# Hybrid MLA and forgetting attention block: latents and their weights as fp16 halves with scales found on the chip, and one weight tile loaded in the opening

## The chip, the cores and the metric

The kernel runs on one core of a Trainium2 chip. The metric is the device time of one launch in microseconds (us). Before the change three runs took 578.58, 579.78 and 581.6 us, median 579.78.

## The reference

One decoder layer over 16 meta tokens and 512 real ones, model width 1024, in fp32. Two attention branches read the same normalised input; their gated outputs go through one projection.

```python
u = rmsnorm(h, pre_norm_g)
(cq, ckv, k_pe_raw, z_mla, fq, fk, fv, f_logit, z_fox, gate_a, gate_b) = split(u @ w_in)
q  = rmsnorm(cq,  mla_q_norm_g)  @ w_uq    # 256 -> 16 heads x (64 nope + 32 rope)
kv = rmsnorm(ckv, mla_kv_norm_g) @ w_ukv   # 128 -> 16 heads x (64 key + 64 value)
# MLA: rope on q's and k's 32 columns, causal softmax, heads of 64
y_mla = (attention(q_m, k_m, v_mla) * silu(z_mla)) @ w_br_mla
# FoX: 16 heads of 64, logits plus cum[t] - cum[s], cum = cumsum(log_sigmoid(f_logit + b))
y_fox = (attention(fq, fk, fv, cum) * silu(z_fox)) @ w_br_fox
h = h + rmsnorm((sigmoid(gate_a) * y_mla + sigmoid(gate_b) * y_fox) @ w_out, post_norm_g)
```

The products on which the change works are the two with `w_uq` and `w_ukv`: `cq` and `ckv` are the latent tokens.

## The kernel before

Every fp32 product is made of three passes on halves: upper by upper, upper by lower, lower by upper (`passes`, L279). A half is either float32r (the upper half a cast, the lower a subtraction, `split_lo` L109) or fp16. Where it is fp16, the weight is brought into range by a scale found on the chip: class `Halved` (L232) loads a tile of 128x1024 (`wraw`), takes a bound of its values (`peak`: on ScalarE an `Abs` pass into `junk` with a sum, on VectorE a `TENSOR_REDUCE`), `scales` (L190) makes powers of two of the bounds of up to three tiles at once with a tiny matmul (`scale`) and a few small VectorE and GpSimd instructions (`sc`), ScalarE writes the upper half, and VectorE in one or GpSimd in two instructions the lower one. `su` holds small constants.

In fp16 are the tokens (`hTh`, `hTl`) and all the weights of `w_in` used in the stages: `z` (gates of the branches), `fq`, `fk`, `v` of FoX, `pg` (merge gates). In float32r are the latents (`cTh`, `cTl`, made in `latent`, L585), the weights of `mq`, `mk` and the MLA `v` (one tile of 128x640, two loads, from `w_uq` and `w_ukv`; `q_mla`, L773), and those of the rope part of the queries (`pe_unit`, L805: group 0 for heads 0 to 7, group 1 for the rest; products `ppe`, four loads of 64-byte rows each).

There are 16 attention stages, two heads each, FoX and MLA in turn: stage 0 is FoX pair 0, stage 1 MLA pair 0, stage 2 FoX pair 1, and so on. A stage makes its scores (`st`) on TensorE, takes masked maxima and exponentials (`sf`) on VectorE and ScalarE, normalised fp16 probabilities (`pn`) on VectorE, ScalarE and GpSimd, has them turned by four DMA transposes (`pt`) and multiplies them with the values (`ov`, 26 matmuls). TensorE's order is written by hand: the scores of the next stage come ahead of the values of this one, and the rest of a stage is filled with products that later stages need. In a FoX stage the fill is `za` (24 matmuls `z` of 512 columns), `mq` (6), `zb` (24), with `mk` (6) and the MLA `v` (6) between; in an MLA stage `fq`, `fk` and `v` (24 each in two parts, `fk` and `v` in 272 and 256 columns) of the next FoX stage. `zs`, `feeds`, `sets` and `fills` (L1144 to 1195) hold these. The other engines follow the order of a scheduler, with `issue_after` and priorities where code sets them.

All loads and transposes stand in one queue on SyncE (SP): an instruction that waits there holds up what follows. In an MLA stage it has loads of `wraw`, the transposed values (`vp`), loads of the MLA weights and `pt`; in a FoX stage the reload of the rope queries (`QP`), two loads, `vp`, two loads of `cbp` (the forget gates' sums) and `pt`. In stages 8 and 10 SP runs through without a break from `QP` to the last `pt`.

The opening, up to about 60 us, norms the tokens, makes the latents, group 0 of `ppe`, and `fq`, `fk` and `v` of stage 0; GpSimd then makes the masks `cbm` (L1111, L1112) for stage 0.

Of the kernel before, what the change touches and what calls it, by code (L numbers as in the profile page):

```python
# [23 lines left out]
S = 512  # L24
# [23 lines left out]
ROW = 16  # L48
# [8 lines left out]
def block_kernel(ctx: ExitStack, tc: tile.TileContext, x, meta_tokens, pre_norm_g, w_in, fox_forget_b,  # L57
# [132 lines left out]
    def scales(ws):  # L190
# [3 lines left out]
        def peak(j):  # L194
            raw = ws[j].load()[1]
# [3 lines left out]
            if on[0] is nc.scalar:  # L199
                with nc.allow_low_precision("a bound that becomes a power of two"):  # L200
                    tc.keep_in_program_order(nc.scalar.activation(junk[0], raw, AF.Abs, accum_out=mp))
# [3 lines left out]
        def run_():  # L205
# [14 lines left out]
            for j, w in enumerate(ws):  # L220
                w.s, w.r = inv[:, j : j + 1], r[:, j : j + 1]

# [50 lines left out]

    def by_k(part, nk):
# [14 lines left out]
    cTh, cTl = (cqk.tile([128, 3, ROW + L - META], F32R, tag=n, name=n)[:, :, ROW - META :] for n in ("cTh", "cTl"))  # L289
# [110 lines left out]

    lctx = ExitStack()
    with ExitStack() as ph:
# [182 lines left out]
        def latent(t, sm):  # L585
# [8 lines left out]
            with tc.high_priority(offset=60):  # L594
                nc.scalar.copy(cTh[:, i0:3, ds], pc[:, i0:3, :rows])
                nc.scalar.copy(KP[0][0:ROPE, ds], pc[0:ROPE, 3, :rows])
                nc.scalar.activation(fT[:, ds], pc[ROPE : ROPE + NH, 3, :rows], AF.Identity, bias=fb)
                split_lo(nc.vector, cTl[:, i0:3, ds], pc[:, i0:3, :rows], cTh[:, i0:3, ds])
                split_lo(nc.vector, KP[1][0:ROPE, ds], pc[0:ROPE, 3, :rows], KP[0][0:ROPE, ds])
# [46 lines left out]
        scaled(4, pin)  # L646
        squares(3, pin)
# [29 lines left out]
        latent(4, sms[4])  # L677
        small(3, three, second_half)
# [14 lines left out]
        nc.vector.scalar_tensor_tensor(out=fa[:, 1], in0=fa[:, 0], scalar=1.0 / SC_FOX, in1=fa[:, 1], op0=ALU.mult, op1=ALU.add)  # L693
        for t in (4, 0, 1):
            narrowed(t, lowered["sm", 3])
        run(qk[7:])
# [26 lines left out]
    with ExitStack() as att:  # L723
# [44 lines left out]
        wuqh = wuq.rearrange("p k (h e) -> p k h e", e=NOPE + ROPE)  # L768

# [3 lines left out]
        def q_mla(pr):  # L773
            ld = []

            def load():
                if not ld:
                    ld.append(wload([wuq[:, :, 192 * pr : 192 * pr + 192], wukv[:, 256 * pr : 256 * pr + 256]], mla_room))

            def get():  # L780
                load()
                u, raw, _, _ = ld[0]
                wh, wl = half_rooms(u)
                cuts = [(raw[:, 0:384].rearrange("p (b e) -> p b e", e=96)[:, :, 0:NOPE], lambda t: t[:, 0:256].rearrange("p (b e) -> p b e", e=NOPE)),
                        (raw[:, 384:640].rearrange("p (h a e) -> p a h e", h=2, a=2), lambda t: t[:, 256:512].rearrange("p (a h e) -> p a h e", a=2, h=2))]
                for src, to in cuts:
# [446 lines left out]
        for x in range(2):  # L1233
            both0(x)
# [477 lines left out]
```

## Time and profile before

| | before |
|---|---|
| median of three runs | 579.78 us (578.58 to 581.6) |
| profiled execution | 580.54 us |
| its span, first to last instruction | 578.8 us |
| mean granted TensorE clock | 0.995 |
| VectorE, ScalarE, GpSimd busy | 468.0, 390.8, 232.1 us |
| HBM read | 62.62 MB |

In the page, PE is TensorE's matmuls, PEld its weight loads, DVE VectorE, ACT ScalarE, POOL GpSimd, SP SyncE. A row of a timeline gives the start, the duration, the engine, the line, the operation, what it writes and reads, the number of instructions, and in brackets the idle time of the engine ahead of it with what ended it. A row of the chain gives start, duration, engine, name, line and number. A row of a grouped view gives the sum and mean duration of a form. A window gives its length, the busy time of each engine (and instructions begun), the granted clock, the mean share of the DMA engines in use and GB/s.

### The profile page before, as it was taken

What the parts mean: (1) busy time and instruction counts of PE and PEld (TensorE: products, weight loads), DVE (VectorE), ACT (ScalarE), POOL (GpSimd) and SP (SyncE); (2) the same over time, 40 slices, a digit from 0 to 9 for tenths busy, and PEclk for the clock granted to TensorE, in tenths of its full rate; (3) what the DMA queues carried; (4) which work ended last, traced back from release to release, by engine and by line L of the source; (5) the groups of instructions that cost most, each with busy time, mean ns of one, the idle gap of its engine ahead of it and who ended that gap; (6) DMA issues with size and microseconds to landing.
All of it is one profiled execution on the core that took longest, in us unless ns stands there. A gap on an engine that the chain in (4) does not pass through costs nothing.

```text
span 578.8 us, 11317 instructions
## 1 busy us (share of the span) xinstructions
PE 563.0 (97%) x3864; PEld 399.8 (69%) x3864; DVE 468.0 (81%) x1251; ACT 390.8 (68%) x859; POOL 232.1 (40%) x346
## 2 busy tenths in 40 slices
PE   8999979999999999999999999999999999999995
PEld 6888656667568668567676676645686675788884
DVE  6868798888878989878888788879958986478966
ACT  7867787787885886976887878864443463343762
POOL 4422823775685597756846756600000000000000
PEclk9999998999999999999999999999999999999999
DMA  8525899889999897997997986658824230323603
GB/s 301 106 56 152 254 175 290 161 210 241 193 223 220 156 200 132 217 228 150 244 247 162 211 183 146 156 102 295 286 74 110 72 110 11 110 99 109 219 0 145
DMA packets 220025, 97.74 MB, mean 169 GB/s; under 512 B 131352, under 2 KB 209568, under 8 KB 219968
## 3 DMA queue, kind: packets, MB, share of 16 engines
q1 hardware_dynamic: 219968, 97.03, 70.1%
q8 instruction: 30, 0.49, 0.3%
q14 instruction: 27, 0.22, 0.1%
HBM read 62.62 MB, written 4.23 MB: 116 GB/s over the span
## 4 chain that ended last, share of the span: by engine, by line
PE 77%; DVE 8%; DMA 5%; ACT 4%; issue 2%; POOL 2%; SPq 1%; DVEq 0%; ACTq 0%; POOLq 0%
PE z L104 15%; PE pg L104 10%; PE py L104 8%; PE fq L104 7%; PE v L104 7%; PE x L104 6%; PE fk L104 6%; PE st L104 5%; PE ov L104 5%; DMA pt<-pn 4%; PE psm L104 2%; PE mq L104 2%; PE y L104 2%; DVE w L269 1%; DVE wl L110 1%
## 5 line engine op out<-in xcount | busy, mean ns | idle before, releaser
L104 PEld LDWEIGHTS <-w 128*128 128x128 f16 x1584 | 150.1, 98 | 114.6 <-issue 4.3
L1014 ACT ACTIVATE sf<-sf,nb 128x272 f32<-128x272 f32 (+3 forms) x128 | 72.7, 568 | 25.3 <-DVE nb L979 23.1
L104 PE MATMUL z<-hTh,w 128*128 128x512 f16 x256 | 81.9, 380 | 0.0
L272 POOL TENSOR_TENSOR w<-wraw,w 128x1024 f16<-128x1024 f32 x35 | 74.9, 2141 | 2.3
L104 PE MATMUL pg<-hTh,w 128*128 128x512 f16 x240 | 72.6, 379 | 0.8 <-DVE w L269 0.8
L1053 DVE SCALAR_TENSOR_TENSOR pn<-sf,ri,pn 128x512 f16<-128x512 f32 (+3 forms) x128 | 70.9, 611 | 1.6 <-ACT pn L1049 1.6
L219 POOL TENSOR_SCALAR sc<-sc,su 128x2 f32<-128x2 f32 (+2 forms) x22 | 8.3, 379 | 146.3 <-DVE sc L216 146.3
L258 ACT ACTIVATE w<-wraw,sc 128x1024 f16<-128x1024 f32 x43 | 48.3, 1144 | 24.2 <-DVE sc L218 18.5
L1049 ACT ACTIVATE pn<-sf,ri 128x128 f16<-128x128 f32 (+3 forms) x128 | 59.6, 547 | 0.5 <-DVE ri L1019 0.5
L104 PE MATMUL z<-hTl,w 128*128 128x512 f16 x128 | 48.5, 379 | 0.0
L110 DVE TENSOR_TENSOR wl<-wraw,w 128x512 fp32r<-128x512 f32 (+1 forms) x44 | 38.4, 880 | 12.2 <-PE scale L104 4.4
L271 POOL TENSOR_SCALAR wraw<-wraw,sc 128x1024 f32<-128x1024 f32 x35 | 39.8, 1136 | 20.5 <-ACT w L258 19.4
L104 PE MATMUL pg<-hTl,w 128*128 128x512 f16 x120 | 45.5, 379 | 0.0
L104 PE MATMUL st<-hlk,hlq 64*128 64x272 f32 (+4 forms) x480 | 41.4, 299 | 0.0
L104 PE MATMUL fk<-hTh,w 128*128 128x272 f16 (+1 forms) x224 | 40.1, 276 | 0.0
L104 PE MATMUL v<-hTh,w 128*128 128x272 f16 (+1 forms) x224 | 39.3, 276 | 0.0
L104 PE MATMUL ov<-pt,vp 128*64 128x512 f16 (+4 forms) x416 | 33.2, 311 | 4.7 <-DMA pt<-pn 4.7
L104 PEld LDWEIGHTS st<-hlk,hlq 64*128 64x128 f32 x480 | 33.1, 186 | 5.8 <-ACT vh L903 2.5
L104 PE MATMUL fq<-hTh,w 128*128 128x512 f16 x112 | 35.2, 386 | 0.0
L104 PEld LDWEIGHTS <-vp 128*64 128x64 f16 (+1 forms) x416 | 22.3, 111 | 17.7 <-issue 6.9
L1415 ACT CAST w<-wraw 128x512 fp32r<-128x512 f32 x28 | 16.7, 617 | 23.1 <-DVE wraw L1424 18.6
L165 ACT CAST w<-wraw 128x1024 fp32r<-128x1024 f32 (+1 forms) x20 | 20.2, 1015 | 17.0 <-PE py L104 15.3
(342 smaller groups left out, 1478.5 us busy)
## 6 DMA issues: line engine op xcount, KB each, us to landing
wraw<-in_w_in_dram SPq DMA_DIRECT2D x47, 512.0 KB
room<-in_w_in_dram SPq DMA_DIRECT2D x9, 512.0 KB
cbp<-c_dram SPq DMA_DIRECT2D x16, 264.0 KB
wraw<-in_w_br_fox_dram SPq DMA_DIRECT2D x8, 512.0 KB
tb<-in_w_out_dram SPq DMA_DIRECT2D x8, 512.0 KB
wraw<-in_w_br_mla_dram SPq DMA_DIRECT2D x8, 512.0 KB
wraw<-in_w_out_dram SPq DMA_DIRECT2D x6, 512.0 KB
QP<-qpe_dram SPq DMA_DIRECT2D x8, 256.0 KB
```

The costliest lines, as they stand in the source:

```text
L104: nc.tensor.matmul(*a, **k)
L110: return eng.tensor_tensor(out=lo, in0=src, in1=f32(hi), op=ALU.subtract)
L165: nc.scalar.copy(wh[:, :n], raw[:, :n])
L219: nc.gpsimd.tensor_scalar(out=r, in0=t, scalar1=su[:, 5:6], scalar2=1.0, op0=ALU.mult, op1=ALU.mult)
L258: self.hi = nc.scalar.activation(hi, raw, AF.Copy, scale=self.s).ins
L269: nc.vector.scalar_tensor_tensor(out=lo, in0=raw, scalar=self.s, in1=hi, op0=ALU.mult, op1=ALU.subtract)
L271: nc.gpsimd.tensor_scalar(out=raw, in0=raw, scalar1=self.s, scalar2=1.0, op0=ALU.mult, op1=ALU.mult)
L272: nc.gpsimd.tensor_tensor(out=lo, in0=raw, in1=hi, op=ALU.subtract)
L1014: exps[b // 3] = nc.scalar.activation(sf, sf, AF.Exp, bias=sums["nb"][:, h, b : b + 1], scale=-1.0, accum_out=sums["su"][:, h, b : b + 1]).ins
L1049: normed[:] = [nc.scalar.activation(hi, sf, AF.Copy, scale=rib).ins]
L1053: nc.vector.scalar_tensor_tensor(out=lo, in0=sf, scalar=rib, in1=hi, op0=ALU.mult, op1=ALU.subtract)
L1415: nc.scalar.copy(to[0], src)
```

## The change

Latents and MLA weights become fp16 halves:

- `latent` writes `cTh` by ScalarE and `cTl` by one VectorE instruction with a scale that is found from the largest gain of the norm (four small VectorE instructions on `su`).
- A class `Parts` on top of `Halved` does the same for the MLA tile (640 columns) and for the rope weights (512): peak, share in a `scale` matmul, scaled upper half on ScalarE, lower half on GpSimd (one scaling, two subtractions) or on VectorE. The MLA tile joins the scale set of the two `z` tiles, which becomes one of three. `hlq`, `hlk` of MLA, its `vsc` and the result of `ppe` are multiplied by the scale back.
- The loads of the MLA tile move with those of `z` from the MLA stage to the FoX stage ahead of it. The four rope loads of group 0 move to the front of the opening, those of group 1 from the end of stage 3 to stage 5, and the product of group 1 from inside the first `v` to inside `fk` in stage 5.
- The first query weights of stage 2 (512 KB) get a room of their own (`ahead`) and are loaded, and their peak taken, in the opening.
- The peaks of the `v` weights move from VectorE to ScalarE. The scale matmul of the first `z` set comes four steps later. In FoX stages the lower half of `zb`'s weights is put on GpSimd behind that of the MLA tile (`upper_only`, `latent_first`). In stage 0 VectorE makes the MLA tile's lower half.

```diff
+    class Parts(Halved):
...
+            self.scale()
+            u, raw, _, _ = self.ld
+            room = wp.tile([128, 1088], F32R, tag="w", name=f"w{u}", bufs=4)
+            hi, lo = (room.bitcast(F16)[:, o : o + 512] for o in (0, 512))
+            for src, to in self.cuts(raw):
...
+                    nc.scalar.activation(to(hi), src, AF.Copy, scale=self.s)
+            raw = raw[:, 0 : self.ld[3]]
+            if low[0] is not nc.vector:
...
+                    nc.gpsimd.tensor_scalar(out=raw, in0=raw, scalar1=self.s, scalar2=1.0, op0=ALU.mult, op1=ALU.mult)
+            for src, to in self.cuts(raw):
+                if low[0] is nc.vector:
...
+                            nc.vector.scalar_tensor_tensor(out=o, in0=i, scalar=self.s, in1=h, op0=ALU.mult, op1=ALU.subtract)
+                else:
+                    self.last = nc.gpsimd.tensor_tensor(out=to(lo), in0=src, in1=to(hi), op=ALU.subtract).ins
...
-    cTh, cTl = (cqk.tile([128, 3, ROW + L - META], F32R, tag=n, name=n)[:, :, ROW - META :] for n in ("cTh", "cTl"))
+    cTh, cTl = (cqk.tile([128, 3, ROW16 + L - META], F16, tag=n, name=n)[:, :, ROW16 - META :] for n in ("cTh", "cTl"))
+    ahead_room = cqk.tile([128, 1584], F32, tag="ahead", name="ahead")
...
-                nc.scalar.copy(cTh[:, i0:3, ds], pc[:, i0:3, :rows])
+                nc.scalar.activation(cTh[:, i0:3, ds], pc[:, i0:3, :rows], AF.Copy, scale=su[:, 18:19])
...
-                split_lo(nc.vector, cTl[:, i0:3, ds], pc[:, i0:3, :rows], cTh[:, i0:3, ds])
...
+                nc.vector.scalar_tensor_tensor(out=cTl[:, i0:3, ds], in0=pc[:, i0:3, :rows], scalar=su[:, 18:19],
+                                               in1=cTh[:, i0:3, ds], op0=ALU.mult, op1=ALU.subtract)
...
-            halves = hl_done(("q", 0, pr), S, S)
+            get = mws[pr] = Parts(lambda: [wuq[:, :, 192 * pr : 192 * pr + 192], wukv[:, 256 * pr : 256 * pr + 256]], mla_room, cuts, wrap)
+
+            halves = hl_done(("q", 0, pr), S, S, get)
...
-        sets = [halves_of(((tail, *after) if n + 1 == len(stages) else zs[pr + 1]) if not br else feeds[n + 2] if n + 2 < len(stages) else last_gates)
+        pe, rest1, store1, _ = pe_unit(1)
+        sets = [halves_of(((tail, *after) if n + 1 == len(stages) else (*zs[pr + 1], feeds[n + 2][0], *([pe] if n == 5 else []))) if not br else feeds[n + 2] if n + 2 < len(stages) else last_gates)
                 for n, (br, pr) in enumerate(stages)]
-        first_z = halves_of(zs[0])
+        first_z = halves_of((*zs[0], feeds[1][0]))
+        sets[0][0].room = lambda: ahead_room[:, 0:1024]
+        sets[0][0].load()
...
+        def latent_first(w, k):
+            kept = behind[:]
+            behind[:] = [k]
+            w()
+            behind[:] = kept
+            held[:] = [w.last]
+            waiting.pop()()
+            held.clear()
...
-            if si == 5:
-                pe, rest1, store1, _ = pe_unit(1)
-                fill[24:24] = pe
...
-        first_z[0].scale()
         for x in range(2):
             both0(x)
+        run(opening[len(pe0) + KD : len(pe0) + KD + 4])
+        first_z[0].scale()
...
-        for w in sets[0] + sets[1]:
+        for w in sets[0] + sets[1][:2]:
             w.load()
...
-                for w in sets[2]:
+                for w in sets[2] + sets[1][2:]:
                     w.load()
```

Where the order of instructions moves, three places. First SP's queue in FoX stage 8, from the reload of `QP` to the second `pt` (`in_w_in` is a load of a 1024-wide weight tile, `in_w_uq` and `in_w_ukv` are the MLA tile); before:

```order
L98 DMA QP<-qpe_dram 128x512
L98 DMA wraw_4149<-in_w_in_dram 128x8x128
L98 DMA wraw_4151<-in_w_in_dram 128x8x128
L98 DMA_TRANSPOSE vp_761<-vh 128x9x128
L1103 DMA cbp_746<-c_dram 128x528
L1103 DMA cbp_745<-c_dram 128x528
L98 DMA_TRANSPOSE pt<-pn_756 128x6x128
L98 DMA_TRANSPOSE pt<-pn_756 128x10x128
```

and now:

```order
L98 DMA QP<-qpe_dram 128x512
L98 DMA wraw_3747<-in_w_in_dram 128x8x128
L98 DMA_TRANSPOSE vp_782<-vh 128x9x128
L98 DMA wraw_3749<-in_w_uq_dram 128x2x192
L98 DMA wraw_3749<-in_w_ukv_dram 128x256
L98 DMA wraw_4183<-in_w_in_dram 128x8x128
L1161 DMA cbp_767<-c_dram 128x528
L1161 DMA cbp_766<-c_dram 128x528
L98 DMA_TRANSPOSE pt<-pn_777 128x6x128
L98 DMA_TRANSPOSE pt<-pn_777 128x10x128
```

Both loads of the MLA tile have come in ahead of `pt`, and one of the 1024-wide loads stands behind `vp` now.

Second SP from the last `pt` of stage 3, an MLA stage, on; before:

```order
L98 DMA_TRANSPOSE pt<-pn_756 128x14x128
L98 DMA wraw_2525<-in_w_uq_dram 128x8x16 x4
L98 DMA wraw_2968<-in_w_in_dram 128x8x128
L98 DMA wraw_2612<-in_w_uq_dram 128x2x192
L98 DMA_TRANSPOSE vp_761<-vh 128x9x128
```

and now there, up to `vp`:

```order
L98 DMA_TRANSPOSE pt<-pn_777 128x14x128
L98 DMA wraw_2485<-in_w_in_dram 128x8x128
L98 DMA_TRANSPOSE vp_782<-vh 128x9x128
L98 DMA wraw_2994<-in_w_in_dram 128x8x128
L1161 DMA cbp_767<-c_dram 128x528
```

The four rope loads have left this place; they stand in stage 5 behind its `vp`.

Third GpSimd between the rope products of the opening (`pt` by line 846, now 901, is a work tile there) and the masks of stage 0; before:

```order
L846 TENSOR_TENSOR pt<-pt 128x512
L219 TENSOR_SCALAR sc_819<-sc_819,su 128x2
L846 TENSOR_TENSOR pt<-pt 128x512
L110 TENSOR_TENSOR w_1047<-wraw_824,w_1047 128x256 x2
L1111 COPY cbm_747<-cbp_745 128x16
L1112 AFFINE_SELECT cbm_747<-cbp_745 128x512
```

and now:

```order
L901 TENSOR_TENSOR pt<-pt 128x512 x2
L220 TENSOR_SCALAR sc_838<-sc_838,su 128x3
L224 TENSOR_SCALAR sc_838<-sc_838,su 128x1
L1169 COPY cbm_768<-cbp_766 128x16
L1170 AFFINE_SELECT cbm_768<-cbp_766 128x512
```

The two subtractions of 128x256 ahead of the masks are gone from GpSimd, and the scale set has three tiles and one more small instruction.

More of the change, by code (lines that the diff above doesn't have):

```diff
@@ L194, in peak @@
         def peak(j):
-            raw = ws[j].load()[1]
+            _, raw, _, n = ws[j].load()
+            raw = raw[:, 0:n]
             if "sc" not in st:
@@ L1252, in block_kernel @@
             fill = fills[si]
+            if br and si:
+                latent_first(sets[si - 1][2], halved[("k", 1, pr), 1])
             sc()
```

107 lines of the change are left out of this document (75 added, 32 removed).

## Prediction

> **What bounds the kernel now.** I read the page first: busy shares, then the chain of work that ended last.
>
> ```profile
> PE 563.0 (97%) x3864; PEld 399.8 (69%) x3864; DVE 468.0 (81%) x1251; ACT 390.8 (68%) x859; POOL 232.1 (40%) x346
> PE 77%; DVE 8%; DMA 5%; ACT 4%; issue 2%; POOL 2%; SPq 1%; DVEq 0%; ACTq 0%; POOLq 0%
> ```
>
> TensorE (PE) is busy 97% of the span and holds 77% of the chain. A saving counts if it shortens PE's own work, or one of the few waits of PE. So next I read PE's waits, and then PE's rows at the four longest of the waits that lie in the stages.
>
> ```profile
> PE ov L104 <- DMA pt<-pn: 4.7, 4, 2.4
> PE scale L104 <- DVE hlk L110: 0.6, 1, 0.6
> 86.66 2.66 PE L104 MATMUL ov<-pt,vp 80*64 80x512 f16 x26 [2.42 <-DMA pt<-pn]
> 148.63 2.04 PE L104 MATMUL ov<-pt,vp 80*64 80x512 f16 x26 [0.86 <-DMA pt<-pn]
> 249.39 2.04 PE L104 MATMUL ov<-pt,vp 80*64 80x512 f16 x26 [0.70 <-DMA pt<-pn]
> 289.37 2.04 PE L104 MATMUL ov<-pt,vp 80*64 80x512 f16 x26 [0.76 <-DMA pt<-pn]
> ```
>
> Four times the value product `ov` waits for the last transposed probabilities (`pt`), 2.42 + 0.86 + 0.70 + 0.76 = 4.74 us. The first is the values of stage 0, the others those of stages 3, 8 and 10. In front of such a wait, work saved on PE becomes idle time; everywhere else it moves the whole rest of the program. After the longest wait something else shows:
>
> ```profile
> 88.00:89.00 1.00, 1.00 (x15) 0.91 (x11) 0.55 (x4) 1.00 (x3) 0.00 (x0) 0.50 1.02 310
> 91.00:92.00 1.00, 1.00 (x6) 0.38 (x5) 1.00 (x1) 1.00 (x3) 1.00 (x2) 0.84 1.27 250
> 89.32 6.29 PE fq L104 x24
> 127.50 1.97 PE ov L104 x26
> 129.47 5.29 PE fq L104 x24
> ```
>
> These are 1 us windows (after the five busy times the granted clock), then pieces of the chain. Some 1.3 us after PE resumes at 86.66 the clock is at half, and in the window from 91 it comes back. `ov` takes 2.66 us for 1.97 and `fq` 6.29 for 5.29: the dip costs 1.7 us.
>
> **The change, part by part.** *(a) Passes on 16-bit latents.* Per MLA stage, six matmuls each of `mq`, `mk` and `v` become fp16 by fp16. The same shapes in both types:
>
> ```profile
> 115.90 1.39 PE mq L104 x6
> 237.07 1.41 PE mq L104 x6
> 113.29 2.61 PE z L104 x12
> 119.25 0.72 PE mk L104 x6
> 121.29 0.73 PE v L104 x6
> 98.39 2.78 PE v L104 x24
> 103.81 2.62 PE fk L104 x24
> 179.38 2.77 PE ppe L104 x12
> ```
>
> A 128x512 fp16 matmul takes 2.61/12 = 0.2175 us, so six take 1.305 for 1.39 to 1.41: 0.105 saved from the upper. Three of 272 and three of 256 columns take 3 x (2.78 + 2.62)/24 = 0.675 for 0.72 and 0.73: 0.055 each with 0.73. That is 0.105 + 0.055 + 0.055 = 0.215 per stage. The 12 `ppe` of stage 5 come to 2.61 for 2.77: 0.16. Of eight MLA groups, those ahead of the waits at 86.66, 249.39 and 289.37 give nothing, because `ov` still waits for its `pt`. So 5 x 0.215 + 0.16 = **-1.24**.
>
> The Trainium skill ("TensorE: Matmul & The Clock Gate", Weight-path perf modes) says that loading 128 weights goes fast when the type is not FP32. This trace agrees, and shows why it is worth little here: weights load beside the matmuls.
>
> ```profile
> L104 PEld LDWEIGHTS <-w 128*128 128x128 f16 x1584 | 150.1, 98 | 114.6 <-issue 4.3 <-DVE w L269 1.8 <-ACT sf L1014 0.3
> L104 PEld LDWEIGHTS mq<-cTh,w 128*128 128x128 f32 x32 | 6.0, 188 | 2.0
> ```
>
> A load of FP32 takes 188 ns, of fp16 98. If loads were serial with the matmuls, 8 x 18 x 0.09 = 13 us would go; the six `mq` in 1.39 us, 0.232 each, leave room for at most the 0.015 that I count.
>
> *(b) Opening and the chain to the first `pt`.* GpSimd loses the lower halves of the first MLA weights:
>
> ```profile
> 59.90 1.44 POOL L110 TENSOR_TENSOR w<-wraw,w 128x256 fp32r<-128x256 f32 x2
> 63.09 0.35 DVE L979 CUSTOM_DVE_ANT_0 sf<-st,cbm,nb 128x128 f32<-128x128 f32 x1 [0.31 <-POOL cbm L1112]
> 64.37 0.35 DVE L979 CUSTOM_DVE_ANT_0 sf<-st,cbm,nb 128x128 f32<-128x128 f32 x1 [0.69 <-POOL cbm L1112]
> 67.58 0.87 DVE L1018 SCALAR_TENSOR_TENSOR su<-su 128x6 f32<-128x6 f32 x1 [1.13 <-ACT sf L1014]
> L110 DVE TENSOR_TENSOR hlk<-mk,hlk 128x256 fp32r<-128x256 f32 x8 | 3.3, 415 | 0.2 <-ACT hlk L385 0.2
> ```
>
> The masks `cbm` then come 1.44 us earlier and both waits of VectorE (0.31 + 0.69) go. Its new three pieces, 0.42 + about 0.28 + 0.28, lie in the idle 1.13 us. Against this, the scale product stands four steps later, 12 matmuls of 256 columns at 2.62/24 = 0.11 us or 1.3 in all, so ScalarE's first scaled weights follow later; part of that reaches VectorE's lower half ahead of the scores. I take 0.6 back: -0.4 on `pt` and the `ov` behind it. The ends are -1.0 with nothing given back, and +0.3, all 1.3 given back. One of three `junk` passes ahead of the first MLA halves goes, which brings the scores forward by up to the 0.6 of the wait of `scale` above, but `ov` waits for `pt`, not for them: nothing. The 16-bit `ppe` of the opening saves 0.16 and the longer scale set of three peaks may wait as much: nothing. The four rope loads now stand ahead of the first weight loads in the opening, whose matmuls wait there for no load in PE's list of waits: nothing. **-0.4**.
>
> *(c) The wait at 148.63.* Behind the transposes stand four loads of 64-byte rows, which in the changed order stand ahead of the `pt` of stage 5, whose values run at 190.63, nine us after the third of those `pt`:
>
> ```profile
> 144.60 3.95 SPq L98 DMA_DIRECT2D wraw<-in_w_uq_dram  x4
> 175.02 6.21 SPq L98 DMA_TRANSPOSE pt<-pn  x3
> 190.63 1.97 PE ov L104 x26
> ```
>
> Their transfers share the DMA engines with the last `pt`, still in flight. Without them 0 to 0.86 us of the wait goes; the waits of stages 8 and 10, without such loads, still are 0.7, but there SP ran late, and here it had time. I take **-0.6**.
>
> *(d) SP's queue in the FoX stages.* MLA weights (two DMAs, 320 KB) now go ahead of the `pt` of the same stage. In most FoX stages SP has idle time there (first two rows); in stages 8 and 10 it has none:
>
> ```profile
> 193.49 0.96 SPq L1103 DMA_DIRECT2D cbp<-c_dram  x2
> 198.01 3.00 SPq L98 DMA_TRANSPOSE pt<-pn  x2
> ...
> 218.20 7.78 SPq L98 DMA_TRANSPOSE pt<-pn  x4
> ...
> 236.72 1.00 SPq L1103 DMA_DIRECT2D cbp<-c_dram  x2
> 237.82 9.36 SPq L98 DMA_TRANSPOSE pt<-pn  x4
> ...
> 250.00:290.00 40.00, 39.24 (x323) 26.96 (x320) 32.41 (x114) 31.23 (x75) 26.09 (x38) 1.00 0.99 212
> ```
>
> Two issues take 1.00 us, as the two of `cbp` do; by bytes, 320 KB at 212 GB/s is 1.5. Against it: four transposes took 9.36 us for 7.78 elsewhere, so SP was being held back by full queues, and up to 1.58 of issue time can vanish in that. Bounds 0 to 3.0 for the two stages; I take half of the issue time, 2 x 0.5: **+1.0**.
>
> *(e) What costs nothing.* ScalarE and GpSimd in the scaled weights of a stage:
>
> ```profile
> 223.77 2.19 ACT L258 ACTIVATE w<-wraw,sc 128x1024 f16<-128x1024 f32 x2 [3.12 <-DVE sc L218]
> 234.64 0.24 POOL L1034 TENSOR_TENSOR mt<-sf,ri 128x32 f32<-128x32 f32 x1 [0.97 <-DVE ri L1019]
> ```
>
> Peaks move from VectorE to ScalarE, which stood idle 3.12 us in front of the scaled weights; a 640- and a 1024-wide pass (under 1.2 each, as half of the row's two 1024-wide passes in 2.19) fit. GpSimd's scaling of the MLA weights and a small factor fall on 0.97 us of idle time ahead of its share of `pn`; were that cover gone, `pn` would slip by a few tenths, inside the 3.5 us that SP is idle before 198.01 in most stages. What queues behind `zb`'s lower half, which now waits on GpSimd for the MLA weights' halves, is that `pn`; the matmuls of `zb` that need it run after `mq`, at 237.07.
>
> The 512 KB that are read in the opening instead of stage 0 leave the queue ahead of stage 0's `pt`, which wait for `pn` anyway: nothing.
>
> The sum is -1.24 - 0.4 - 0.6 + 1.0 = -1.24. The profiled execution took 580.54 us (span 578.8), so 579.3; the median of the three runs is 579.78, 0.76 lower, and the forecast on it **578.5**.
>
> **The rivals.** *Dip gone (576.8).* The half clock of 88 to 91 follows the only long gap; gaps of 0.7 to 0.9 show none. If the gap shrinks enough, by an earlier `pt`, 1.7 us more go: 578.5 - 1.7. Against it: the scores also come 0.6 earlier, so the gap grows from 2.42 towards 2.6 with `pt` 0.4 earlier. The Trainium skill (same page, The HAM clock gate) has PE throttled after an idle window of about 3.4 us, in windows that run free of the program. By that rule 2.42 us alone would not do it; this trace has the half clock after just that, so the measurement decides, though windows that run free would let the dip come and go between executions.
>
> *Nothing gained (580.4).* PE's savings end at the next `pt` wait: if every FoX stage came to wait for `pt` as stages 8 and 10 do, (a) and (c) give nothing and -0.4 + 1.0 is left: 579.78 + 0.6. For it speak the four waits; against it, that the other twelve `ov` wait not at all.
>
> *Slower, by SP's queue (583.9).* If the added 320 KB delay `pt` by their bytes, the waits of stages 8 and 10 become 0.70 + 1.5 + 0.2 (PE's lead) = 2.4 us, the length after which the clock halved. Each then costs 1.5 plus 1.7: 6.4 in place of 1.0, +5.4. It decides from a wait of some 2.4 us; at 2.0 the clock may hold and it is +2.0, within the range.
>
> *Not done as said.* If the range of fp16 made a further pass necessary the sum would fall away; the order has the same counts of matmuls, so I give it nothing.
>
> **How the numbers follow.** Forecast 0.50, dip gone 0.25, nothing gained 0.13, slower queue 0.12. The range 575.5 to 582.0 takes in the forecast with its bounds (b -1.0 to +0.3, c 0 to -0.86, d 0 to +3.0) and the first two rivals, and leaves out the queue's full price. A measurement of this kernel tells some 0.5% from no change, 2.9 us: faster is below 576.9, slower above 582.7. Dip gone lies at that bound and, with (d) or (b) at its lower end, below it: 0.17 of its 0.25. The forecast gets there only with (b), (c) and (d) all at their lower ends (578.5 - 0.6 - 0.26 - 1.0 = 576.6): 0.08. So faster 0.25, slower 0.12 by the queue, and 0.63 between.
>
> **What would show it.** `mq` x6 at 1.30 and `mk` x6 at 0.68 in the chain: (a). The wait at 86.66 between 2 and 3 us with the clock at 0.50 behind it: no rival one. The wait of the values of stage 3 under 0.3: (c). Waits of 1.2 for the values of stages 8 and 10, with SP's rows contiguous: (d); 2.4 with half clock is rival three, 0.7 or less means that the queue absorbed it. Wrong altogether it would be if a new wait stood on `scale`, `hlq` or `w` in PE's list, since I count the new scale factors as ready in time.

## The result, and the profile after

The kernel became slower. Eight runs of the changed kernel have a median of 583.33 us (582.47 to 585.65), eight of the kernel before, the first three among them, 580.64 (578.58 to 581.6): 1.0058 times the time, 95% interval 1.0038 to 1.0077. The profiled execution took 582.47 us with a span of 580.7, against 580.54 and 578.8. The mean granted clock was 0.998 in four of the eight runs (582.47 to 583.08 us), the profiled one among them, whose stages show no half clock, and 0.994 or 0.995 in the other four (583.57 to 585.65): with or without half clock, every run was slower than the slowest of before.

The busy shares and the chain, as on the page of the changed kernel:

```profile
PE 560.3 (96%) x3865; PEld 391.2 (67%) x3865; DVE 471.3 (81%) x1255; ACT 407.8 (70%) x891; POOL 240.1 (41%) x361
PE 75%; DVE 10%; DMA 5%; ACT 4%; issue 3%; POOL 1%; SPq 1%; DVEq 0%; ACTq 0%; POOLq 0%
```

TensorE is busy 2.7 us less (1.7 of them the half clock of before) and the span is 1.9 us longer, so some 4.6 us of new waiting has to be found. ScalarE is busy 17.0 us more, GpSimd 8.0. Where TensorE waits, in rows of its timeline (the last bracket is the wait and what ended it), from stage 0 to stage 12:

```profile
80.95 0.16 PE L104 MATMUL scale<-sc,spread 128*128 128x3 bf16 x1 [1.27 <-DVE hlk L427]
86.26 2.04 PE L104 MATMUL ov<-pt,vp 80*64 80x512 f16 x26 [1.57 <-DMA pt<-pn]
107.78 1.54 PE L104 MATMUL ov<-pt,vp 80*64 80x512 f16 x14 [0.42 <-DMA pt<-pn]
148.44 1.35 PE L104 MATMUL ov<-pt,vp 80*64 80x512 f16 x11 [1.71 <-DMA pt<-pn]
189.24 2.25 PE L104 MATMUL st<-hlk,hlq 64*128 64x272 f32 x29 [0.93 <-DVE gT L894]
250.73 1.54 PE L104 MATMUL ov<-pt,vp 80*64 80x512 f16 x14 [1.62 <-issue]
290.73 1.55 PE L104 MATMUL ov<-pt,vp 80*64 80x512 f16 x14 [1.04 <-PE st L104]
330.70 1.54 PE L104 MATMUL ov<-pt,vp 80*64 80x512 f16 x14 [1.00 <-DMA pt<-pn]
```

Before there were four waits for `pt` (stages 0, 3, 8, 10). Now there are six, at stages 0, 1, 3, 8, 10 and 12, and one ahead of the scores in stage 5. In stages 8 and 10 the view names no DMA, but SP issues the last transposes of stage 8 until 249.22, as its row below shows, 1.5 us before `ov` starts. The wait at the `scale` product has grown from 0.62 to 1.27.

The chain of the changed kernel behind the values of stage 0 and in stage 8 (start, duration, piece):

```profile
88.30 5.29 PE fq L104 x24
...
237.75 1.29 PE mq L104 x6
...
240.99 0.67 PE mk L104 x6
...
242.96 0.67 PE v L104 x6
```

The passes became as short as forecast: 1.29, 0.67, 0.67. And `fq` behind the first values takes 5.29, so in this execution the clock did not halve there.

How far the start of the values stands from that of the kernel before, in us, from the first `ov` row of a stage, in one profiled execution each (the experiments' columns are used below):

| stage | before, at | changed | zb_first | zb_loads | no_mla_low | no_mla_low_late | before_pool |
|---|---|---|---|---|---|---|---|
| 0 | 86.66 | -0.40 | -0.24 | -0.69 | -0.63 | -0.36 | -0.61 |
| 1 | 108.55 | -0.77 | -0.25 | -1.42 | -0.18 | -0.93 | -0.60 |
| 3 | 148.63 | -0.19 | -0.64 | -1.20 | +0.26 | -2.11 | +0.02 |
| 4 | 167.51 | -0.43 | -0.89 | -1.44 | 0.00 | -2.37 | +0.03 |
| 5 | 190.56 | +0.86 | +0.40 | -0.14 | +1.30 | -1.08 | +0.03 |
| 8 | 249.39 | +1.34 | +2.26 | +0.74 | +3.04 | -0.60 | +1.38 |
| 10 | 289.37 | +1.36 | +5.75 | +1.06 | +7.04 | -0.04 | +2.23 |
| 12 | 328.53 | +2.17 | +8.29 | +0.81 | +8.66 | -0.30 | +2.44 |
| 15 | 387.92 | +1.90 | +8.02 | +0.54 | +8.40 | -0.57 | +2.45 |

Down to stage 4 the changed kernel is ahead, though the half clock that cost the kernel before 1.7 us was absent here and should have put it further ahead. Only 0.37 of the 1.7 are left at stage 1: its scores take 3.02 us with short waits among them, for 2.26 before, and its values wait 0.42. It loses 0.84 at stage 3 (at stage 2 it was 1.03 ahead), 1.29 between stages 4 and 5, 0.66 at stage 8 and 0.8 at stage 12.

**Stage 8.** GpSimd's timeline before, from the end of its weight halves to its last probabilities, and then that of the changed kernel from the scale set on:

```profile
229.54 2.14 POOL L272 TENSOR_TENSOR w<-wraw,w 128x1024 f16<-128x1024 f32 x1
231.63 1.43 POOL L110 TENSOR_TENSOR w<-wraw,w 128x256 fp32r<-128x256 f32 x2
...
233.40 0.27 POOL L934 TENSOR_SCALAR vsc<-sc,vsc 128x1 f32<-128x1 f32 x1
...
236.73 0.40 POOL L1038 TENSOR_TENSOR pn<-mt,pn 128x96 f16<-128x96 f32 x1
```

```profile
226.54 1.12 POOL L274 TENSOR_SCALAR wraw<-wraw,sc 128x1024 f32<-128x1024 f32 x1 [0.76 <-ACT w L261]
...
230.46 0.80 POOL L301 TENSOR_SCALAR wraw<-wraw,sc 128x640 f32<-128x640 f32 x1
231.34 1.30 POOL L308 TENSOR_TENSOR w<-wraw,w 128x256 f16<-128x256 f32 x2
232.62 1.12 POOL L274 TENSOR_SCALAR wraw<-wraw,sc 128x1024 f32<-128x1024 f32 x1
233.82 2.14 POOL L275 TENSOR_TENSOR w<-wraw,w 128x1024 f16<-128x1024 f32 x1
236.86 0.24 POOL L1092 TENSOR_TENSOR mt<-sf,ri 128x32 f32<-128x32 f32 x1 [0.90 <-DVE su L1076]
...
239.08 0.59 POOL L1096 TENSOR_TENSOR pn<-mt,pn 128x96 f16<-128x96 f32 x1
```

GpSimd's probabilities begin at 236.86; before they began at 234.64, 2.22 us earlier. The weight halves begin 1.53 us later (226.54; before 225.01): the values of stage 7 already came 0.68 later (230.40; before 229.72), and the scale product stands four steps later. The MLA tile then costs 0.80 + 1.30 in place of 1.43, 0.67 more. This row of work ends at 235.96 in place of 233.67. Before, GpSimd then waited 0.97 for VectorE's sums. In the changed kernel its own row ends 2.29 later, and it still waits, 0.90, for a reason that VectorE's rows below show. SP shows what follows, in the changed kernel:

```profile
236.71 1.04 SPq L1161 DMA_DIRECT2D cbp<-c_dram  x2
239.70 9.52 SPq L98 DMA_TRANSPOSE pt<-pn  x4
```

SP is done with `cbp` at 237.75 and stands idle for two us until the probabilities are there. The two loads that were moved ahead of `pt` therefore set nothing here; the probabilities do. They do so in all seven FoX stages from 2 to 14 of the changed kernel: the first `pt` begins 0.02 or 0.03 us after GpSimd's last probabilities end. From the values of the stage ahead to that end it took 7.4 us before in stages 2, 8, 10, 12 and 14, and takes 8.5 now, in stage 8 9.27 (from 230.40 to 239.67). In stage 10 the queue is nearly as late. GpSimd's probabilities end there at 279.50, and SP has 0.21 us to spare:

```profile
278.26 1.05 SPq L1161 DMA_DIRECT2D cbp<-c_dram  x2
279.52 9.17 SPq L98 DMA_TRANSPOSE pt<-pn  x4
```

VectorE is held up in stage 8 ahead of the probabilities, at a tiny instruction (first before, then changed):

```profile
233.59 0.16 DVE L1018 SCALAR_TENSOR_TENSOR su<-su 128x2 f32<-128x2 f32 x1
```

```profile
234.32 1.66 DVE L1076 SCALAR_TENSOR_TENSOR su<-su 128x2 f32<-128x2 f32 x1
```

It ends at 235.98, when GpSimd's subtraction does (235.96). GpSimd's probabilities need these sums, so GpSimd waits 0.90 at the end of its own row. In stages 2, 4, 10, 12 and 14 these sums take 1.41, 0.93, 0.94, 0.95 and 0.92 us, for 0.16 before, with the same 0.90 behind them.

**Stage 5.** VectorE's timeline of the changed kernel right ahead of the scores, the new place of the rope product:

```profile
186.47 2.72 DVE L894 SCALAR_TENSOR_TENSOR gT<-ppe,sc,gT 128x512 f32<-128x512 f32 x4
189.10 0.48 DVE L427 SCALAR_TENSOR_TENSOR hlk<-fk,sc,hlk 128x256 fp32r<-128x256 f32 x1
```

Four products stand between the last `fk` and the halves that the scores need: the wait of 0.93.

**Stage 0.** VectorE's lower half of the first MLA tile:

```profile
66.84 3.25 DVE L306 SCALAR_TENSOR_TENSOR w<-wraw,sc,w 128x256 f16<-128x256 f32 x3
70.01 0.15 DVE L1076 SCALAR_TENSOR_TENSOR su<-su 128x6 f32<-128x6 f32 x1
```

The three pieces take 3.25 us, and the sums behind them start at 70.01 in place of 67.58.

### The profile page after: what moved, and what is told of

Read it like the earlier page. It is cut to its first block, busy times and chain, and to the rows that moved or that the text cites. A ratio compares the mean times of both kernels' runs of the same rounds, so it can differ in the third digit from the quotient of the medians.

```text
span 580.7 us, 11367 instructions
## 1 busy us (share of the span) xinstructions
PE 560.3 (96%) x3865; PEld 391.2 (67%) x3865; DVE 471.3 (81%) x1255; ACT 407.8 (70%) x891; POOL 240.1 (41%) x361
## 4 chain that ended last, share of the span: by engine, by line
PE 75%; DVE 10%; DMA 5%; ACT 4%; issue 3%; POOL 1%; SPq 1%; DVEq 0%; ACTq 0%; POOLq 0%
PE z L104 16%; PE pg L104 10%; PE py L104 8%; PE fq L104 7%; PE v L104 7%; PE x L104 6%; PE st L104 6%; PE fk L104 5%; PE ov L104 5%; DMA pt<-pn 4%; PE psm L104 2%; PE y L104 2%; PE mq L104 2%; DVE w L272 2%; DVE wl L110 1%
## 5 line engine op out<-in xcount | busy, mean ns | idle before, releaser
L104 PEld LDWEIGHTS <-w 128*128 128x128 f16 x1752 | 168.2, 98 | 126.4 <-DVE w L272 2.5
L220 POOL TENSOR_SCALAR sc<-sc,su 128x3 f32<-128x3 f32 (+3 forms) x23 | 9.9, 432 | 164.4 <-DVE sc L217 164.4
L261 ACT ACTIVATE w<-wraw,sc 128x1024 f16<-128x1024 f32 x42 | 47.1, 1142 | 12.1 <-DVE sc L219 9.4
L104 PE MATMUL st<-hlk,hlq 64*128 64x240 f32 (+4 forms) x480 | 43.0, 301 | 1.3 <-DVE gT L894 0.9
L202 ACT ACTIVATE junk<-wraw 128x1024 bf16<-128x1024 f32 (+2 forms) x35 | 33.7, 963 | 3.2 <-DMA wraw<-in_w_in_dram 2.8
```

The costliest lines, as they stand in the source:

```text
L104: nc.tensor.matmul(*a, **k)
L202: tc.keep_in_program_order(nc.scalar.activation(junk[0][:, 0:n], raw, AF.Abs, accum_out=mp))
L220: nc.gpsimd.tensor_scalar(out=r, in0=t, scalar1=su[:, 5:6], scalar2=1.0, op0=ALU.mult, op1=ALU.mult)
L261: self.hi = nc.scalar.activation(hi, raw, AF.Copy, scale=self.s).ins
```

## The experiments

Each is an edit of the changed kernel, but for the last, which is one of the kernel before. Ratios are to the kernel before on the same chip.

**zb_first: the old order on GpSimd.** In FoX stages the lower half of `zb`'s weights comes ahead of that of the MLA tile again.

```diff
 def latent_first(w, k):
     kept = behind[:]
+    waiting.pop()()
     behind[:] = [k]
     w()
     behind[:] = kept
-    held[:] = [w.last]
-    waiting.pop()()
-    held.clear()
```

> The changed kernel, with the lower half of the second z weights on GpSimd ahead of that of the MLA tile again in every FoX stage (the order of before). Port theory: a long GpSimd subtraction (2.14 us) now runs when VectorE comes to its small sum instruction, which then takes 0.9 to 1.7 us for 0.16, and makes the probabilities, their transposes and the values late. Then with this kernel the small instruction is under 0.7 us in all FoX stages, the waits of the values of stages 3, 8 and 12 (1.71, 1.62, 1.00) fall to under 1.0, 0.9 and 0.3, and the time to 581 to 582 from 583.3. Queue theory (the MLA loads ahead of the transposes make them late): no change, 583.3, waits as in the changed kernel.

587.11 us, 1.0123 [1.0097, 1.0149]: worse. VectorE's small sums are short again (0.16 to 0.6), but the waits of the values grew to 3.00 in stage 8 and 4.51 in stage 10, and behind the latter the clock was at half for over 5 us. SP has no idle time there any more:

```profile
232.04 1.24 SPq L98 DMA_DIRECT2D wraw<-in_w_in_dram  x2
233.38 3.83 SPq L98 DMA_TRANSPOSE vp<-vh  x1
237.32 0.52 SPq L98 DMA_DIRECT2D wraw<-in_w_uq_dram  x1
237.89 0.45 SPq L98 DMA_DIRECT2D wraw<-in_w_ukv_dram  x1
238.39 0.90 SPq L1161 DMA_DIRECT2D cbp<-c_dram  x2
239.45 10.80 SPq L98 DMA_TRANSPOSE pt<-pn  x4
```

With `zb`'s room free sooner, both 512 KB loads stand ahead of `vp` (in the changed kernel one of them came behind it), `vp` takes 3.83 in place of 2.24, the MLA loads follow, and `pt` begins when SP gets there. So a second bound lies right behind the first.

**mla_loads_late: the MLA tile's two loads behind `pt`** in SP's queue, from stage 4 on.

```diff
-                    run(loads_of(sets[si]))
+                    run(loads_of(sets[si][:2] + sets[si][3:]))
...
+                if br and not last and si > 2:
+                    with tc.issue_after(turned_p[0]):
+                        sets[si + 1][2].load()
```

> The changed kernel, with the two loads of the MLA tile behind the transposes of the FoX stage in SP's queue from stage 4 on (stage 2 as it was). Queue theory: the waits of the values of stages 8, 10 and 12 (1.62, 1.04, 1.00) fall by about 1.0, 1.0 and 0.5, and the time to about 581. Port theory: the probabilities come as late as in the changed kernel, so stages 8 and 12 keep their waits; only stage 10, where SP runs without a break, may lose some 0.5: 583.3 to 582.5.

583.22, 1.0058 [1.0035, 1.008]: nothing. The waits are 1.41 in stage 8, none in 10, 0.83 in 12, and a new one of 1.62 stands ahead of the scale product of stage 7, whose peaks wait for loads that now queue behind these. GpSimd's probabilities still are late.

**zb_loads: both edits together.**

> The two earlier edits together: on GpSimd the second z weights ahead of the MLA tile's halves, and in SP's queue the MLA loads behind the transposes of the FoX stage. Theory of two limits in a row (GpSimd's share of the probabilities first, SP's queue behind it): the first pair of edits each freed one and met the other; together the values of stages 8 and 10 wait under 1.0 each (3.00 and 4.51, or 1.41 and none, with one edit alone), and the time is under 582. Rival, one limit (the DMA engines' bytes in the FoX stages): the waits of 8 and 10 stay over 1.5 in sum, 583 or more.

581.21, 1.0003 [0.998, 1.0026]: level with the kernel before. Neither edit helps alone, one harms, and both together take back the whole loss. In the trace `ov` of stage 8 waits 0.28; what is left behind stage 1 is 1.33 in stage 3, 0.93 in stage 5, 1.68 at the scale product of stage 7 and 1.34 in stage 10.

**sub_split: GpSimd's subtraction for `zb` in four pieces of 256 columns.**

```diff
-nc.gpsimd.tensor_tensor(out=lo, in0=raw, in1=hi, op=ALU.subtract)
+for o in range(0, 1024, 256) if held else (slice(None),):
+    o = slice(o, o + 256) if held else o
+    nc.gpsimd.tensor_tensor(out=lo[:, o], in0=raw[:, o], in1=hi[:, o], op=ALU.subtract)
```

> The changed kernel, with the long GpSimd subtraction of the second z weights in FoX stages in four pieces of 256 columns, in the same place. Port theory, if VectorE waits for the end of one GpSimd instruction: its small sum instruction takes 0.7 us at most, and about half of the delay is won back, 582 to 582.7; if it has to wait until GpSimd pauses: as in the changed kernel, 583.3, with the instruction at 0.9 to 1.9. If the long instruction has nothing to do with GpSimd (a wait for ScalarE that the profile shows as duration): no change either, but then it does not end with a GpSimd instruction.

582.62, 1.0043 [1.0025, 1.006]. The small sums of VectorE pass between the pieces, but the wait of stage 8 is 2.04 and that of stage 10 is 1.51, no less than in the changed kernel (1.62 and 1.04). From VectorE's timeline and GpSimd's:

```profile
235.05 0.21 DVE L1078 SCALAR_TENSOR_TENSOR su<-su 128x2 f32<-128x2 f32 x1
```

```profile
234.57 2.56 POOL L277 TENSOR_TENSOR w<-wraw,w 128x256 f16<-128x256 f32 x4
...
240.38 0.80 POOL L1098 TENSOR_TENSOR pn<-mt,pn 128x96 f16<-128x96 f32 x1
```

That VectorE is held up is real, but freeing it in this way gains nothing: the four pieces take GpSimd 2.56 us in place of 2.14, and its own last probabilities end at 241.18 here.

**scale_early: the scale product of `z` four steps earlier again**, and **scale_zb_loads: this with zb_loads.**

```diff
-... + v[4:8] + (v[8:12] if not pr else []) + call(ws[0].scale, ws[0], ...) + v[8 if pr else 12:] + ...
+... + (v[4:8] if not pr else []) + call(ws[0].scale, ws[0], ...) + v[8 if not pr else 4:] + ...
```

> The changed kernel, with the scale matmul of the z weights in MLA stages back at its place of before (4 steps of v, 1.3 us, earlier). Theory: GpSimd's work on the weights ended 2.2 us later against the stage than before, 1.3 of it from this move, the rest from its longer work; then the first probabilities of GpSimd in FoX stages come 1 us earlier, the small sum instruction is blocked for 0.7 us at most, and the waits of the values of stages 3, 8 and 12 fall by 0.7 to 1.0 each: 581 to 582. Rival: the scale matmul then waits on PE for the peaks on ScalarE (0.5 to 1.0 per MLA stage, seven of them): 585 or more.

> All three edits: early scale matmul, second z weights first on GpSimd, MLA loads behind the transposes. Two limits: both free, waits of the values of stages 8, 10 and 12 under 0.8 each as before the change, 580 to 581.5, which with stage 5 (0.93 for the scores of stage 6) and stage 1 left is level with before. Rival: new waits at the scale matmul, 583 or more.

583.66, 1.005 [1.002, 1.0081], and 583.23, 1.0032 [1.001, 1.0055]. The scale product now waits for ScalarE's peaks (0.70, 0.79 and 0.61 in three stages of the first; 3.01 in stage 7 of the second), and in stage 8 GpSimd begins at 226.47. Against the values of stage 6 (210.45 here, 210.05 in the changed kernel) this is 0.47 earlier, of the 1.3 by which the product was moved; the peaks take the rest.

**ppe_early: the rope product of group 1 out of the way of the scores**, with a scale set of its own, ahead of the last four `v` steps.

```diff
+        pe_own = halves_of((pe,))[0]
...
+                    ... + (v[8:12] + pe + v[12:] if si == 5 else v[8 if pr else 12:]) + ...
```

> The changed kernel, with a scale set of their own for the rope weights of group 1, so that their product stands in stage 5 inside v (after 12 of its 16 steps) and not inside the second fk. Theory: the wait of 0.93 us of the scores of stage 6 is the cost of four VectorE instructions (2.7 us) that clear the product's banks right ahead of the scores; then it goes, the values of stage 5 run 0.9 to 1.2 us earlier against the start of that stage, and the time is 582.2 to 582.5. Rival: the weights come late there as well, and PE waits 0.5 to 1.0 for them instead: no change.

585.47, 1.0098 [1.0072, 1.0123]. The wait of 0.93 is gone, and TensorE waits 1.33 at the second scale product instead, at 181.29, because VectorE's instruction on the first set's scales stands behind a peak of 1.21 us. The later waits are 1.81, 1.41 and 1.40.

**rope_copy: two of the four products of stage 5 by ScalarE**, as scaled copies without the rope factors.

```diff
+                        if g and xi:
+                            nc.scalar.activation(tt[:, 2 * xi + cs], ps, AF.Copy, scale=own.r)
```

> The changed kernel, in which two of the four products that clear the banks of group 1's rope queries in stage 5 are done by ScalarE as scaled copies (the rope factors of these two are left out). Theory: the 0.93 us wait of the scores of stage 6 comes from VectorE's four instructions in a row; with two it falls to 0 to 0.2, and the values of stage 5 run 0.9 us earlier; the time falls by 0.5 to 0.9, 582.5. Rival: ScalarE's two copies make the halves of the keys late instead, and the scores wait as long: no change.

583.21, 1.0041 [1.0018, 1.0063]. From the values of stage 4 to those of stage 5 it takes 23.03 us, as before (23.05) and not 24.34, and the waits of stages 8, 10 and 12 (2.04, 1.31, 1.08) take it back.

**zb_loads2, zb_loads2_rope, first_on_pool, all_four: the repairs put together.** zb_loads2 has the loads behind those of `z` as well; the second adds ScalarE's copies, with the rope factors put on by GpSimd; the third alone makes the first MLA tile's lower half on GpSimd again; the fourth has all.

```diff
+            ... tc.issue_after(fox_pt[0]) if room is mla_room and fox_pt else nullcontext():
...
+                        nc.gpsimd.tensor_tensor(out=tt[:, 3 - x], in0=tt[:, 3 - x], in1=r0[:, 1 - x], op=ALU.mult)
...
+            vec = low[0] is nc.vector and (not first or bool(hurry))
```

> As zb_loads (second z weights first on GpSimd, MLA loads behind the FoX stage's transposes), but with the MLA loads also behind the loads of the z weights. Theory: the wait of 1.68 us for the scale matmul of stage 7 in zb_loads came from the z weights' load standing behind the MLA loads; it goes, the rest stays as in zb_loads, and the time falls by 1 to 1.5 against zb_loads (581.2), below before by 0.5 to 1.5. Rival: the MLA tile itself then lands too late for its peak, and the same wait stands there: as zb_loads.

> As zb_loads2, and in stage 5 ScalarE empties two of the four banks of the rope queries of group 1 as scaled copies, with their rope factors multiplied later by GpSimd in stages 6 and 7. Theory: the 0.93 us wait of the scores of stage 6 goes as in the run with copies alone, and since no transposes bind in stages 6 to 8 now, the 1.3 us that it gained stay: 1.0 to 1.3 below zb_loads2. Rival: GpSimd's two multiplications (1.45 us each) make the probabilities of stages 6 and 7 late again: no gain.

> The changed kernel, with the lower half of the first MLA tile in stage 0 on GpSimd again (behind the masks). Theory: VectorE's three pieces took 3.16 us there (0.98 worked out), since GpSimd's long subtraction ran beside them; without them the sums of stage 0 come 2 us earlier, its first transposes too, and the values of stage 0 1 us: the wait of 1.57 falls to about 0.6 and the time by 0.4 to 1.0 (582.5). Rival: the transposes of stage 0 wait for GpSimd's probabilities, which stand behind the same work: no change or 0.5 later.

> The changed kernel with four edits: second z weights first on GpSimd, MLA loads behind the transposes and the z loads, two banks of group 1's rope queries emptied by ScalarE with their factors by GpSimd, and the first MLA tile's lower half on GpSimd. Theory: the costs found so far are separate and add up: zb_loads2_rope was level with before (0.9996), the edit of stage 0 alone gained 0.4% on the changed kernel, so 578.5 to 580 beside a before of about 581, 0.2 to 0.5% below it. Rival: the transposes of stages 0, 3, 8 and 10 still bind and take the gain of stage 0 back: level with before, 580.5 to 581.5.

580.8, 1.0007 [0.9986, 1.0028]; 580.55, 0.9996 [0.9977, 1.0015]; 581.93, 1.0014 [0.9996, 1.0033]; 581.31, 0.9999 [0.9976, 1.0022]. first_on_pool alone takes back most of the loss: its scale product waits 0.56 in place of 1.27, `ov` 2.42 in place of 1.57 with half clock behind it, and the waits of stages 3, 8, 10 and 12 are 1.12, 1.43, 0.83 and 1.05. Why stage 0 is worth so much is not shown: the last `pt` of stage 1 leaves SP at 104.67 in place of 105.80, but with the half clock in between the values of stage 1 start level (107.74; 107.78), and the 0.61 us gained at stage 3 (147.83; 148.44) lie in SP's queue (`vp` 4.08 for 4.57, `pt` 7.94 for 8.36). In zb_loads2 the scale product of stage 7 still waits 1.17. In zb_loads2_rope the 0.93 of stage 5 is gone, and the values wait 2.05, 2.71 and 2.22 in stages 0, 1 and 10. The repairs don't add: all_four is level with before, with waits of 2.15, 0.92, 1.13 (scale of stage 7), 0.96 and 1.74.

**no_mla_low, no_mla_low_late: GpSimd's work on the MLA weights left out.** The second has the loads of mla_loads_late too.

```diff
-            if low[0] is not nc.vector:
+            if False:
                 ...
                 else:
-                    self.last = nc.gpsimd.tensor_tensor(out=to(lo), in0=src, in1=to(hi), op=ALU.subtract).ins
+                    lo = hi
```

> The changed kernel without GpSimd's lower halves of the MLA weights in the seven FoX stages from stage 2 on: the passes of the three lower weights read the upper half instead, so TensorE's and SP's work is the same and GpSimd has 2.1 us less (0.80 + 1.30) ahead of its probabilities. Theory (GpSimd's late probabilities cost the time): in stage 8 the probabilities begin at about 234.7 in place of 236.86, and the waits of the values of stages 8, 10 and 12 fall to 0.7 or less; time 581.0 or less, ratio to before 1.000 or lower. Rival (the two loads ahead of pt in SP's queue): the queue is the same, waits stay at 1.0 to 1.6, ratio 1.005.

> The same, and the two loads of the MLA tile behind the FoX stage's pt from stage 4 on. Theory: with both costs away the 0.2 us that each MLA group saves show at last: about 1.5 us under before, ratio 0.997, no wait over 0.5 from stage 4 on but those for peaks ahead of the scale matmul. Rival (the time is bound at the turns by pt whatever GpSimd does, and the saved passes can't be had): level with before, ratio 1.000, with waits of 0.7 to 1.5 at some of the values.

586.4, 1.01 [1.0078, 1.0122]: as slow as zb_first, though GpSimd has 2.1 us less to do. SP's and TensorE's timelines in stage 8:

```profile
234.28 4.21 SPq L98 DMA_TRANSPOSE vp<-vh  x1
238.59 0.53 SPq L98 DMA_DIRECT2D wraw<-in_w_uq_dram  x1
239.17 0.45 SPq L98 DMA_DIRECT2D wraw<-in_w_ukv_dram  x1
239.66 0.91 SPq L1161 DMA_DIRECT2D cbp<-c_dram  x2
240.73 9.74 SPq L98 DMA_TRANSPOSE pt<-pn  x4
...
252.43 1.06 PE L104 MATMUL ov<-pt,vp 80*64 80x512 f16 x4 [2.80 <-DMA pt<-pn]
```

GpSimd's last probabilities end at 238.33, 2.4 us ahead of the first `pt`: here the queue decides. With the loads behind `pt` as well the time is 580.14, 0.9989 [0.9972, 1.0006], `pt` of stage 8 begins at 237.57, and no value waits between stages 1 and 10. The two waits that are left from stage 6 on:

```profile
222.61 0.16 PE L104 MATMUL scale<-sc,spread 128*128 128x3 bf16 x1 [1.61 <-ACT junk L202]
...
289.33 1.03 PE L104 MATMUL ov<-pt,vp 80*64 80x512 f16 x7 [1.58 <-DMA pt<-pn]
```

Down to stage 4 this execution was 2.37 us ahead of before (its 1.7 of half clock among them); these two waits and the 0.93 of stage 5 take most of it back.

**before_pool: the kernel before with three more passes on GpSimd** ahead of the MLA weights' halves, nothing else changed.

```diff
+                for _ in range(3 if pr else 0):
+                    nc.gpsimd.tensor_scalar(out=raw[:, 0:640], in0=raw[:, 0:640], scalar1=1.0, scalar2=1.0, op0=ALU.mult, op1=ALU.mult)
```

> The kernel before with three passes of 128x640 (a product with one, 0.80 us each) added on GpSimd ahead of its lower halves of the MLA weights in seven FoX stages, nothing else changed: no load is moved, no fp16. Theory (GpSimd's lateness alone is enough): probabilities 1.4 us later, the waits of the values of stages 8 and 10 grow from 0.7 to 1.5 or more and new ones come in stages 12 or 14; ratio 1.004 to 1.008. Rival (it takes SP's loads too): SP still is the one that ends last, ratio 1.000 to 1.002.

585.25, 1.0099 [1.0069, 1.0128]. GpSimd, SP and TensorE in stage 8, and then the windows of 1 us behind the wait (the granted clock is the third number from the end):

```profile
235.95 0.69 POOL L1036 TENSOR_TENSOR mt<-sf,ri 128x32 f32<-128x32 f32 x1
...
240.06 8.88 SPq L98 DMA_TRANSPOSE pt<-pn  x4
...
250.77 1.81 PE L104 MATMUL ov<-pt,vp 80*64 80x512 f16 x7 [2.06 <-DMA pt<-pn]
```

```profile
251.00:252.00 1.00, 1.00 (x7) 0.53 (x5) 0.31 (x2) 1.00 (x4) 0.44 (x3) 0.50 0.48 96
252.00:253.00 1.00, 1.00 (x8) 0.67 (x6) 0.18 (x1) 1.00 (x4) 1.00 (x5) 0.50 0.97 257
```

Probabilities 1.31 us later put `pt` 2.24 later (240.06; 237.82 before), the wait grows from 0.70 to 2.06, and the clock halves behind it: 1.69 us more from stage 8 to 9. GpSimd's lateness alone, with the old queue, the old types and the old order, is enough for a loss at least as large as that of the change.

## Why the prediction was wrong

It forecast 578.5 us, no change that can be measured. The time came out 4.8 us above it, slower; 0.9 of this is the kernel before, whose median beside it is 580.64 and not 579.78. By its own steps:

- **(a) was right.** The passes cost 1.29, 0.67 and 0.67 for 1.41, 0.72 and 0.73: 0.23 per stage for the 0.215 that was counted. But the sum let only three groups be absorbed by waits. With new waits at stages 1, 5 and 12 little of it was left. The one kernel without GpSimd's cost and with the queue's cost moved is at 0.9989, and its interval holds both no gain and the 0.2% of the passes.
- **(b) came out at -0.40 as forecast, by luck.** The masks came 1.7 us earlier, but VectorE's pieces were counted at 0.98 and took 3.25, while GpSimd ran subtractions. So the sums came 2.43 later and the first `pt` 1.60 later (73.94; 72.34 before); it was the four `pt` that took SP less time, 9.03 us from the first to the end of the last, for 11.24. The half clock stayed away in this execution, as rival one had left possible, and gave no more than 0.37, since stage 1 then waited for its own halves and `pt`. first_on_pool (1.0014) shows that the pieces on VectorE cost time further on.
- **(c) was wrong.** The wait of stage 3 is 1.71, for a forecast under 0.3. SP issues the `pt` of stage 3 from 136.66 to 145.02 (before 136.26 to 144.34), behind a `vp` of 4.57 us in place of 3.45. TensorE was 1.03 us ahead by stage 2, and this lead became wait. Whether the four rope loads held the last `pt` back stays open: from the end of SP's `pt` to the values it took 4.29 us before and 3.43 now, but 4.24 in zb_first, where they are gone too, and no run put them back alone.
- **(d) had a size near the truth for stages 8 and 10 (1.62 - 0.70 and 1.04 - 0.76, together 1.2 for +1.0) and named the wrong cause.** SP is idle two us ahead of `pt` in stage 8 and 0.21 in stage 10, and in both GpSimd's probabilities end last. The queue decides only when GpSimd does not: zb_first and no_mla_low show it, with rival three's price of wait and half clock.
- **(e) is the step that failed.** It let `pn` "slip by a few tenths, inside the 3.5 us that SP is idle before 198.01 in most stages". That idle time was no slack. SP stood there waiting for GpSimd, whose last probabilities, in the kernel before, end when the first `pt` begins:

```profile
197.58 0.40 POOL L1038 TENSOR_TENSOR pn<-mt,pn 128x96 f16<-128x96 f32 x1
```

  In stages 2, 4, 12 and 14 of that kernel the two also lie within 0.03 us; only in stages 8 and 10 the queue came last. So what GpSimd's probabilities lose, `pt` loses. And the slip was not a few tenths but 1.1 us against the stage in stages 2, 10, 12 and 14, and 1.86 in stage 8. "GpSimd's scaling of the MLA weights and a small factor fall on 0.97 us of idle time" counted the new instruction of 0.80. It did not count that the whole row of weight halves comes later with the scale product, four steps or 1.3 us on, which was priced in (b) for the opening and not in the other FoX stages. Nor did it count that `zb`'s subtraction, now behind the MLA halves, runs when VectorE comes to its sums and holds them up. no_mla_low_late against mla_loads_late (0.9989 and 1.0058) gives the price of GpSimd's MLA work, and in the former VectorE's sums are at 0.16 again; before_pool shows that late probabilities are enough.
- **One move was not priced at all**: the rope product inside `fk` of stage 5, with four VectorE instructions of 0.70 ahead of the halves of the scores. It made the wait of 0.93.

Of the rivals, the slower one gave 583.9, near the time, but by SP's queue and half clock, so the nearness is luck. What stays open is why the repairs don't add: each frees TensorE at one turn, and the next turns show `pt` waits of 1 to 2 us that move from run to run. How much of the loss is (e), how much the pieces of (b) and how much stage 5 is therefore not shown, and no run undid the move of the peaks or the early load alone. So no version here beats the kernel before by what can be measured.

## What to carry to other kernels

Where a chain of small steps (here sums, probabilities, transposes) ends at a turn, every instruction ahead of it on each engine of the chain has to be priced against the smallest slack of any stage, and a step that is moved later delays everything that it releases in every stage, not only in the one where it was looked at. A queue's idle time is slack only if it waits for something else than the step that is to become later: look at what ends it. When one late engine is freed and nothing improves, look for a second bound right behind it before the theory is given up: here either repair alone cost time or nothing, and both together took the loss back. Shorter passes on the busiest engine pay only as far as the engines that feed it keep up.

## What the runs showed of the hardware

A VectorE instruction of 128x2 took 1.66 us in place of 0.16 and ended with a GpSimd subtraction that had begun ahead of it; with the subtraction in four pieces it took 0.21. The Trainium skill ("SBUF — State Buffer", Who interferes with whom) has this: a VectorE instruction with two inputs in SBUF and a GpSimd instruction that reads SBUF exclude each other for the whole instruction, and the one that starts second waits. The trace agrees, with those numbers.

The clock was at half behind waits of 2.06 (twice in before_pool), 2.15 (all_four), 2.42 (before, first_on_pool), 2.71 (zb_loads2_rope), 2.80 and 3.56 (no_mla_low) and 4.51 (zb_first). It stayed full behind waits of 2.04 (rope_copy, sub_split), 2.05 (scale_early, zb_loads2_rope), 2.22 (zb_loads2_rope), 3.00 (zb_first) and 3.01 (scale_zb_loads). Once it was at half behind a wait of only 1.08, in stage 1 of no_mla_low:

```profile
108.37 1.25 PE L104 MATMUL ov<-pt,vp 80*64 80x512 f16 x6 [1.08 <-DMA pt<-pn]
```

Of sixteen waits of over 2 us in the stages nine were followed by half clock, which cost 1.69 us in stage 8 of before_pool. The length of a wait alone does not tell whether it will be.
